# Prompt key and value rows of a hybrid decoder step stored from GpSimd's queue in place of the sync queue

## The chip, the cores and the metric

The kernel runs on one core of one Trainium2 chip. It is one launch of one inference step. The metric is the device time of the launch in microseconds (us): the median of several executions, 2409.1 us before the change (three runs, 2408.01 to 2414.72). One further execution was recorded by the profiler; the rows quoted below are from it. It took 2395.49 us.

The engines are called as in the profile: PE is TensorE (matrix products and transposes), DVE is VectorE, ACT is ScalarE, POOL is GpSimd and SP is SyncE. SP does no arithmetic here: it issues transfers (DMAs). POOL does both, in one stream of instructions: arithmetic, and the issue of its own transfers.

## The reference

The reference is one layer of a decoder for 256 prompt tokens and 8 x 4 new tokens of running samples. One input projection feeds two groups of heads (an RWKV-7 recurrence, and sparse attention with compressed, selected and window branches); an output projection and a layer norm follow, and then a mixer that picks experts by product keys, with a second layer norm. What matters here is that the keys and values of the prompt are outputs too:

```python
cuts = [D_NSA + i * NSA_KV_COLS for i in range(7)]
q, kc, vc, ksl, vsl, kw, vw, gl = jnp.split(xn, cuts, axis=-1)
kvh = lambda t: t.reshape(B, T, NSA_KV_HEADS, HEAD_DIM)
new_cmp = jnp.stack([kvh(kc), kvh(vc)], axis=2)
new_sel = jnp.stack([kvh(ksl), kvh(vsl)], axis=2)
new_win = jnp.stack([kvh(kw), kvh(vw)], axis=2)
...
return out, new_cmp, new_sel, win_pad[:, -n_keep:]
```

For each of the three branches a token has a row of 2 x 4 x 64 = 512 floats (keys, then values). For the prompt that is 3 x 256 rows; a block of 128 rows is 256 KB.

## The kernel before, in words

The projection makes the keys and values with columns in the partition dimension (tiles KT and KVT). `kv_rows` turns them into rows: for a token block t and a branch u it does four PE transposes into a PSUM bank (L590), one ACT copy of the bank to an SBUF tile of the ring `wraw` (L592; the ring has four buffers, which the weights of the projection use too), for the selected and the window branch a POOL copy of the values to VS or VW (L594), which the prompt's attention reads later, and the store of the row block to its output (L598). Blocks t = 0 and 1 are the prompt: 2 x 3 stores, six in all. The block of the samples (t = 2) goes out in small pieces at L602.

`kv_rows` is run by `attention_columns` and `new_keys`, in a weave with the second block of the prompt's RWKV steps (L1625). The weave is the order in which the program is written. The order in which each engine executes is chosen afterwards, when the kernel is built, by a scheduler that lays out all engines together by a timeline of its own; only some instructions are pinned (`keep_in_program_order`, `issue_after`). Each engine then runs its own list strictly in order, and an instruction that waits holds all that is behind it on its engine. Every transfer also takes one of eight completion semaphores, in turn, from a set of its kind: one set for SP's queue, one for POOL's. Before it is issued, the transfer that had that semaphore last must have landed.

Names that the prediction uses, in the order of time:

- L455, `gather`: POOL issues an indirect load of 128 rows. `co` tiles are blocks of the samples' compressed and selected cache (512 KB each), `cw` and `rows` are expert rows.
- L517, L522: POOL builds Qb, the samples' queries. L1190 and L1219: POOL's part in the RWKV steps of the prompt.
- L236, L1203, L1251, L1257 on SP: a table of constants (CT), the prompt's RWKV state going out, and the samples' RWKV inputs and states (S0T) coming in.
- From L1649 the samples' attention (`sample_attention`, 20 units: for each, key transposes L925, scores L944, softmax transposes L969, output product L988) is woven with the samples' RWKV steps (state transposes L1262 and L1349, products L1276, state update L1332 to L1344, with the POOL product `uvm` at L1339). It ends at about 746 us. The buffers of the gathered blocks come free when L988 of their unit has run.
- L1712 is the output projection. Its weights are split in a high and a low part (wh, wl; L1705 is the low one), and DVE adds its result to x (L1720). The first layer norm follows on DVE: statistics (L1721, L1770), the inverse root (L242 to L247), shift and scale (L1773), eight normed tiles (L1777), whose transposes on PE (L1780) open the query projection (L1873). Between these, DVE does L1600, products of gathered expert rows with the samples' tokens, and behind them L1796, gain and offset of the norm.

## Time and profile before

| | |
|---|---|
| median of three runs | 2409.1 us (2408.01 to 2414.72) |
| the profiled execution | 2395.49 us |
| its span (first to last instruction) | 2393.7 us |
| clock granted to PE, mean of the span | 0.967 of full speed |
| busy share of PE, DVE, POOL, ACT | 93%, 73%, 54%, 34% |
| SP's queue, POOL's queue | 341.93 MB and 338.78 MB |
| the six stores of L598 | 520.4 to 539.6 us, 1.5 MB |
| PE busy from 520 to 546 us | 25.86 of 26.00 us |
| PE busy from 546 to 746 us | 172.09 of 200.00 us |

The profile is one execution. A row of the timeline has a start, a duration, engine, line, operation, "output<-inputs" and, in brackets, how long the engine was idle just before and which instruction or transfer ended that idle time. A row of the waits has the waiting engine and line, then what it waited for, then the sum of the waits, their number and the longest. An x with a number behind a row is the number of instructions put together in it. Times are in us, durations of single instructions in groups are in ns. The profiled execution is 13.6 us faster than the median of the runs; differences that are worked out within the profile are therefore compared with its own time.

### The profile page before, as it was taken

The numbers are of one execution on the slowest core, as the hardware profiler recorded it, in microseconds if no ns is written. First come the engines' busy times: TensorE is split into PE (matmuls) and PEld (weight loads), VectorE is DVE, ScalarE is ACT, GpSimd is POOL, SyncE is SP. The second block draws the span as 40 slices with busy tenths as digits, with TensorE's granted clock in tenths as the row PEclk, the third lists the DMA queues.
The fourth block names the chain that finished last, engine by engine and source line by source line (L and its number), as shares of the span: only waits on it lengthen the run. The fifth ranks groups of instructions, "written<-read, shape, count | busy, mean of one in ns | idle before, by whom it ended". The sixth has DMA issues, their size and how long they took to land.

```text
span 2393.7 us, 42400 instructions
## 1 busy us (share of the span) xinstructions
PE 2222.6 (93%) x15564; PEld 1859.8 (78%) x15564; DVE 1758.0 (73%) x4041; ACT 824.4 (34%) x1609; POOL 1297.8 (54%) x1342
## 2 busy tenths in 40 slices
PE   7989999898989998699999999997998999999996
PEld 7877889896555665488888888886777888887885
DVE  5789866555664536889677776566877899998888
ACT  3433222223443433211111111113776444444343
POOL 5678522323454204467656654564442788876772
PEclk9999999998998998899999999998999999999998
DMA  7877985448667997799899999996663999999994
GB/s 218 234 228 244 268 238 169 130 140 257 215 238 264 292 321 257 275 354 376 314 375 374 377 391 345 386 403 219 187 196 109 346 356 362 362 363 349 354 357 177
DMA packets 311024, 683.42 MB, mean 286 GB/s; under 512 B 82238, under 2 KB 184576, under 8 KB 309888
## 3 DMA queue, kind: packets, MB, share of 16 engines
q1 hardware_dynamic: 229600, 341.93, 42.7%
q0 software_dynamic: 81216, 338.78, 39.2%
q8 instruction: 123, 2.02, 0.3%
q14 instruction: 85, 0.70, 0.1%
HBM read 665.04 MB, written 23.88 MB: 288 GB/s over the span
## 4 chain that ended last, share of the span: by engine, by line
PE 75%; DMA 8%; DVE 7%; POOL 3%; issue 3%; ACT 2%; SPq 1%; DVEq 0%; POOLq 0%; ACTq 0%
PE pb L2127 20%; PE ph L1919 19%; PE pj L424 8%; PE pj L1873 5%; PE px L1965 3%; PE pa L1712 3%; PE pa L1998 2%; DMA co<-in_cache_sel_kv,sidx 2%; PE p L1098 2%; PE pt L1957 2%; PE ss L1540 1%; PE fs L2017 1%; DMA co<-in_cache_cmp_kv,gidx 1%; DMA rows<-in_peer_u_g,gi 1%; PE sa L925 1%
## 5 line engine op out<-in xcount | busy, mean ns | idle before, releaser
L1919 PE MATMUL ph<-Xfd,ur 128*128 128x256 f32 x2304 | 497.6, 379 | 0.0
L1919 PEld LDWEIGHTS ph<-Xfd,ur 128*128 128x128 f32 x2304 | 437.6, 190 | 59.4
L455 POOL DMA_INDIRECT rq<-in_peer_v_g,gi x256 | 379.4, 1482 | 150.8 <-DVE fP L2100 90.0
L455 POOL DMA_INDIRECT rows<-in_peer_u_g,gi x256 | 303.3, 1185 | 202.7 <-DVE rows L1843 126.7
L1843 DVE SCALAR_TENSOR_TENSOR rows<-rows,x1a 128x896 f32<-128x896 f32 x256 | 279.4, 1099 | 141.5 <-DMA rows<-in_peer_u_g,gi 140.7
L424 PE MATMUL pj<-XH,wl 128*128 128x288 f32 (+1 forms) x752 | 230.8, 307 | 14.4 <-DVE wl L419 7.7
L424 PE MATMUL pj<-XH,wh 128*128 128x288 f32 (+1 forms) x752 | 228.6, 304 | 14.0 <-DVE ss L757 7.1
L2100 DVE SCALAR_TENSOR_TENSOR fP<-rq,ge,fP 128x640 f32<-128x640 f32 x254 | 223.9, 881 | 2.5
L424 PE MATMUL pj<-XL,wh 128*128 128x288 f32 (+1 forms) x752 | 225.0, 299 | 0.0
L2127 PE MATMUL pb<-vl,ah 128*128 128x512 f32 (+1 forms) x768 | 206.4, 377 | 0.8
L2127 PE MATMUL pb<-vh,al 128*128 128x512 f32 (+1 forms) x768 | 205.0, 375 | 0.0
L1920 ACT COPY AW<-ph 128x256 f32<-128x256 f32 x128 | 76.5, 614 | 363.9 <-PE ph L1919 351.2
L2127 PE MATMUL pb<-vh,ah 128*128 128x512 f32 (+1 forms) x768 | 186.7, 378 | 13.4 <-ACT vh L2119 10.9
L417 ACT CAST wh<-wraw 128x512 fp32r<-128x512 f32 (+1 forms) x188 | 114.7, 616 | 223.9 <-PE pj L424 160.0
L2127 PEld LDWEIGHTS pb<-vh,ah 128*128 128x128 f32 x768 | 144.8, 195 | 35.6 <-ACT vh L2119 13.9
L478 DVE SCALAR_TENSOR_TENSOR CA<-co,wbc,CA 128x256 f32<-128x256 f32 x248 | 136.5, 588 | 47.8 <-DMA co<-in_cache_cmp_kv,gidx 47.7
L424 PEld LDWEIGHTS pj<-XH,wl 128*128 128x128 f32 (+1 forms) x752 | 142.9, 190 | 26.5 <-DVE wl L419 12.1
L2127 PEld LDWEIGHTS pb<-vl,ah 128*128 128x128 f32 x768 | 144.6, 194 | 22.9 <-DVE vl L2120 3.8
L2127 PEld LDWEIGHTS pb<-vh,al 128*128 128x128 f32 x768 | 144.6, 194 | 19.2
L424 PEld LDWEIGHTS pj<-XH,wh 128*128 128x128 f32 (+1 forms) x752 | 143.1, 190 | 20.0 <-DVE ss L757 7.5
L424 PEld LDWEIGHTS pj<-XL,wh 128*128 128x128 f32 (+1 forms) x752 | 143.3, 191 | 1.5 <-issue 1.2
L419 DVE TENSOR_TENSOR wl<-wraw,wh 128x512 fp32r<-128x512 f32 (+1 forms) x141 | 101.3, 727 | 39.4 <-ACT wh L417 39.0
(867 smaller groups left out, 4252.5 us busy)
## 6 DMA issues: line engine op xcount, KB each, us to landing
ur<-in_peer_u_t SPq DMA_DIRECT2D x128, 576.0 KB
wraw<-in_w_in SPq DMA_DIRECT2D x152, 256.0 KB
cw<-in_w_out SPq DMA_DIRECT2D x32, 512.0 KB
wraw<-in_w_out SPq DMA_DIRECT2D x32, 512.0 KB
cw<-in_peer_wq SPq DMA_DIRECT2D x32, 512.0 KB
wraw<-in_peer_wq SPq DMA_DIRECT2D x32, 512.0 KB
wraw<-in_w_in SPq DMA_DIRECT2D x64, 128.0 KB
co<-in_state_win_kv SPq DMA_DIRECT2D x16, 512.0 KB
```

The lines of the kernel that those rows point to most:

```text
L417: sc.copy(wh[:, :, :n], w[:, :, :n])
L419: i_ = en.tensor_tensor(wl[:, :, :n], w[:, :, :n], wh[:, :, :n].bitcast(F32), OP.subtract)
L424: last[2] = pe.matmul(pb[:n, :nt], wi[:, k, :n], xi[(o + k) // 8][:, (o + k) % 8, :nt], start=(o + k == 0 and wi is wh and xi is xh), stop ...
L455: gp.indirect_dma_start(out=dst, out_offset=None, in_=rows_, in_offset=bass.IndirectOffsetOnAxis(ap=ix, axis=0))
L478: ve.scalar_tensor_tensor(d_, x_, w_, d_, op0=OP.mult, op1=OP.add)
L1712: pe.matmul(acc[t], xi[:, e, P * t:P * t + P], wi[:, e, :], start=(k == e == n_ == 0), stop=(k == 6 and e == 1 and n_ == 2))
L1843: i_ = ve.scalar_tensor_tensor(r_, r_, 1.0, X1a[t], op0=OP.mult, op1=OP.mult, accum_out=h_)
L1873: pe.matmul(pq[c][:, :NPR], w[:, k, 128 * c:128 * c + 128], XT[:, 4 * g + k, :], start=(g == k == 0), stop=(g == k == 3))
L1919: mm = pe.matmul(ph[:, :NPR], w[:, e, :], Xfd[:, e, :], start=(e == 0), stop=(e == NDB - 1))
L1920: return mm, sc.copy(AW[:, i1 // 64, :, i1 % 64], ph[:, :NPR])
L2100: ve.scalar_tensor_tensor(fP[t], r_, w_, fP[t], op0=OP.mult, op1=OP.add)
L2127: pe.matmul(acc[3 * t + q][:, :n_], wi[:, P * t:P * t + P], xi[:, 512 * q:512 * q + n_], start=(k == 0 and wi is ah and xi is vh), stop=(k ...
```

## The change

One line: the six stores are issued by POOL in place of SP. What they read, where they write and their size stay the same, and so does the waiting for ACT's copy of the row block.

```diff
             if t < 2:
                 o0 = 256 if u == 2 else 0
                 dst = outs[2 + u][0, 0].rearrange("t a h d -> t (a h d)")
-                sy.dma_start(dst[o0 + t * P:o0 + t * P + P, :], row_)
+                gp.dma_start(dst[o0 + t * P:o0 + t * P + P, :], row_)
             else:
```

In the lists of the engines more moves than the six stores, because the scheduler lays out everything that follows anew. Up to the place of the stores, all lists are the same.

First place, the stores themselves (some 519 to 545 us). POOL's list, a piece of the difference (- before, + now); `co` are gathers, `out` the stores:

```order
+L598 DMA out<-wraw 128x512
+L455 DMA co<-in_cache_sel_kv,sidx 128x1024
 L1190 TENSOR_TENSOR SBD_2479<-Sn,DT 64x4x64
 L1190 TENSOR_TENSOR SBD_3634<-Sn,DT 64x4x64
 L594 COPY vs_85<-wraw 128x256
+L598 DMA out<-wraw 128x512
 L594 COPY vw_87<-wraw 128x256
+L598 DMA out<-wraw 128x512 x2
 L594 COPY vs_86<-wraw 128x256
+L598 DMA out<-wraw 128x512
 L517 MEMSET Qb 128x512
```

The first store stands ahead of the fourth of the four gathers there; the second to fifth stand among the copies of L594, and ahead of Qb's memset. The rows that follow:

```order
-L522 COPY Qb<-QT 64x8x4
 L594 COPY vw_88<-wraw 128x256
-L522 COPY Qb<-QT 64x8x4 x15
+L598 DMA out<-wraw 128x512
+L522 COPY Qb<-QT 64x8x4 x16
 L1219 TENSOR_TENSOR YT_105<-YT_105,st_107 128x512
 L455 DMA co<-in_cache_sel_kv,sidx 128x1024 x10
```

The sixth store stands between the last L594 and the sixteen Qb copies, then L1219 and ten gathers. On SP the same six rows are gone, and the rows around them keep their order.

Second place, the samples' attention (546 to 746 us). PE's list at about 590 to 595 us, a piece of the difference:

```order
-L1276 MATMUL ss<-sS,S0T 64x8 x15
+L1276 MATMUL ss<-sS,S0T 64x8 x2
+L969 MATMUL st<-CT_61,S 128x128 x4
+L1276 MATMUL ss<-sS,S0T 64x8 x12
 L925 MATMUL sa<-CT_61,co 128x128 x6
-L969 MATMUL st<-CT_61,S 128x128 x4
```

The softmax transposes of one unit (L969) now stand ahead of key transposes (L925), where they stood behind them. PE's list at about 705 to 720 us before:

```order
L925 MATMUL sa<-CT_61,co 128x128 x6
L969 MATMUL st<-CT_61,S 128x128 x4
L925 MATMUL sa<-CT_61,co 128x128 x7
L1360 MATMUL ss<-Yq,CT_100 128x256
L925 MATMUL sa<-CT_61,co 128x128 x2
L988 MATMUL sao<-co,pt 32x128 x16
L969 MATMUL st<-CT_61,S 128x128 x4
L944 MATMUL sc<-kt,Qb 32x512 x4
L925 MATMUL sa<-CT_61,co 128x128
L988 MATMUL sao<-co,pt 32x128 x16
L969 MATMUL st<-CT_61,S 128x128 x4
L925 MATMUL sa<-CT_61,co 128x128 x6
```

And the same place now:

```order
L1349 MATMUL ss<-CT_61,S0T 128x128 x4
L988 MATMUL sao<-co,pt 32x128 x16
L969 MATMUL st<-CT_61,S 128x128 x4
L1349 MATMUL ss<-CT_61,S0T 128x128 x8
L988 MATMUL sao<-co,pt 32x128 x16
L969 MATMUL st<-CT_61,S 128x128 x4
L1349 MATMUL ss<-CT_61,S0T 128x128 x4
L1355 MATMUL ss<-Ya,CT_100 128x256
L988 MATMUL sao<-co,pt 32x128 x16
L925 MATMUL sa<-CT_61,co 128x128 x6
```

The state transposes (L1349), which before were all done by then, now stand between the units. POOL's list in the same stage, a piece of the difference; the gathers and the state products of L1339:

```order
 L1339 TENSOR_TENSOR uvm<-UB,CT_100 64x512 x2
 L455 DMA co<-in_cache_sel_kv,sidx 128x1024 x2
+L1339 TENSOR_TENSOR uvm<-UB,CT_100 64x512 x5
+L455 DMA co<-in_cache_sel_kv,sidx 128x1024 x4
 L1339 TENSOR_TENSOR uvm<-UB,CT_100 64x512 x2
 L455 DMA co<-in_cache_sel_kv,sidx 128x1024 x4
-L1339 TENSOR_TENSOR uvm<-UB,CT_100 64x512 x3
-L455 DMA co<-in_cache_sel_kv,sidx 128x1024 x10
+L1339 TENSOR_TENSOR uvm<-UB,CT_100 64x512
+L455 DMA co<-in_cache_sel_kv,sidx 128x1024 x6
```

More products than before now stand ahead of the last fourteen gathers: a run of five, then two and one, where it was two and three.

Third place, the first layer norm (some 994 to 1007 us). DVE's list before, around the inverse root (the rows of L242 to L246 ahead of the last round are between the two pieces):

```order
L1720 TENSOR_TENSOR x_11_9724<-x_11_9724,pa 128x512
L1770 BN_AGGR lnmv<-lnst 128x2
L1721 BN_STATS lnst<-x_11_9724 128x6
L1600 SCALAR_TENSOR_TENSOR cw,shT<-cw,x_10451 128x1024
L1770 BN_AGGR lnmv<-lnst 128x2
L1771 TENSOR_SCALAR lnv<-lnmv 128x2
L1600 SCALAR_TENSOR_TENSOR cw,shT<-cw,x_10451 128x1024
L242 TENSOR_SCALAR ln_t<-lnv 128x2
```

```order
L1600 SCALAR_TENSOR_TENSOR cw,shT<-cw,x_10451 128x1024
L245 TENSOR_TENSOR ln_t<-lnrr 128x2
L246 SCALAR_TENSOR_TENSOR ln_t<-ln_t,lnv 128x2
L1600 SCALAR_TENSOR_TENSOR cw,shT<-cw,x_10451 128x1024
L247 SCALAR_TENSOR_TENSOR lnrr<-ln_t,lnrr 128x2
L1773 SCALAR_TENSOR_TENSOR lnv<-lnmv,lnrr 128x2
L1600 SCALAR_TENSOR_TENSOR cw,shT<-cw,x_10451 128x1024
L1777 TENSOR_SCALAR x_00_9721<-x_00_9721,lnrr,lnv 128x512 x2
```

And now; the inverse root stands between the two pieces without a product in it:

```order
L1720 TENSOR_TENSOR x_01_9722<-x_01_9722,pa 128x512
L1600 SCALAR_TENSOR_TENSOR cw,shT<-cw,x_10451 128x1024
L1721 BN_STATS lnst<-x_01_9722 128x6
L1720 TENSOR_TENSOR x_11_9724<-x_11_9724,pa 128x512
L1600 SCALAR_TENSOR_TENSOR cw,shT<-cw,x_10451 128x1024
L1770 BN_AGGR lnmv<-lnst 128x2
L1721 BN_STATS lnst<-x_11_9724 128x6
L1600 SCALAR_TENSOR_TENSOR cw,shT<-cw,x_10451 128x1024
L1770 BN_AGGR lnmv<-lnst 128x2
```

```order
L247 SCALAR_TENSOR_TENSOR lnrr<-ln_t,lnrr 128x2
L1773 SCALAR_TENSOR_TENSOR lnv<-lnmv,lnrr 128x2
L1600 SCALAR_TENSOR_TENSOR cw,shT<-cw,x_10451 128x1024
L1777 TENSOR_SCALAR x_00_9721<-x_00_9721,lnrr,lnv 128x512 x2
```

Between the last addition to `x_01` (L1720) and the first L1777 there are four products of L1600 where there were five. Over the whole list the first L1777 has 20 of the 64 products ahead of it where it had 24; the last addition to `x_01` has 16 where it had 19.

## The prediction

> **What bounds the kernel now.** The page comes first: its head, and its chain of work that ended last.

> ```profile
> span 2393.7 us, 42400 instructions
> PE 2222.6 (93%) x15564; PEld 1859.8 (78%) x15564; DVE 1758.0 (73%) x4041; ACT 824.4 (34%) x1609; POOL 1297.8 (54%) x1342
> ...
> PE 75%; DMA 8%; DVE 7%; POOL 3%; issue 3%; ACT 2%; SPq 1%; DVEq 0%; POOLq 0%; ACTq 0%
> ```

> TensorE (PE) is busy 93% of the span and holds three quarters of the chain. A change elsewhere pays only where PE waits, so the second view is the table of busy time by stretch. Its columns are the stretch, its length, the busy time of PE, PEld, DVE, ACT and POOL, the clock that PE was granted, the DMA share and GB/s.

> ```profile
> 520.00:546.00 26.00, 25.86 (x385) 22.95 (x384) 10.55 (x22) 5.49 (x11) 8.47 (x26) 1.00 0.39 124
> 546.00:746.00 200.00, 172.09 (x1856) 109.24 (x1854) 123.80 (x446) 81.65 (x208) 79.05 (x86) 0.92 0.70 235
> 900.00:1014.00 114.00, 80.19 (x382) 60.71 (x370) 87.68 (x203) 32.96 (x64) 56.47 (x55) 0.82 0.78 273
> 1014.00:1160.00 146.00, 145.26 (x703) 128.43 (x704) 129.55 (x380) 22.61 (x57) 102.81 (x121) 1.00 0.94 340
> ```

> The six row stores fall in the first stretch. PE is idle for 26.00 - 25.86 = 0.14 us there: nothing in that place can be gained. The second (sample attention and the sample RWKV steps) leaves 200 - 172 = 28 us of PE idle, the third (end of the output projection and the first layer norm) 34 us; in the fourth PE is full again. What PE waited for there, in total, times, longest:

> ```profile
> PE sa L925 <- DMA co<-in_cache_sel_kv,sidx: 7.0, 9, 1.8
> PE sa L554 <- DVE gnt L246: 3.1, 1, 3.1
> PE sa L925 <- DMA co<-in_state_win_kv: 1.6, 1, 1.6
> ...
> PE pa L1780 <- DVE x L1777: 12.7, 1, 12.7
> PE pa L1712 <- DVE wl L1705: 6.9, 4, 3.3
> ```

> The first three rows are waits between 546 and 746, the last two between 880 and 1160. None names a store of L598.

> **The change, part by part.** *What leaves SP.* The instructions of L598 (durations in ns: shortest, median, longest; then first and last start), and the table of SP's waits from 510 to 600 (in total, times, longest):

> ```profile
> L598 SPq DMA_DIRECT2D out<-wraw x6: 332/332/361, 520.4 to 539.6; - x6
> ```

> ```profile
> SPq L598 <- ACT wraw L592: 14.8, 5, 8.7
> SPq L236 <- PE pb L590: 1.7, 1, 1.7
> SPq L1203 <- ACT So L1199: 0.9, 2, 0.5
> ```

> Six issues of 0.33 us, 2.0 us in all, nearly all of it inside the 14.8 us in which SP waits for ACT's row copies anyway. What stands behind them does not come earlier: the load of CT (L236) waits 1.7 us more for the PE transposes of the same rows, and the state stores behind it (L1203) wait for ACT. So SP gains at most the one issue of 0.33 us at 539.6, and I put this at 0.

> *What POOL gets.* POOL's timeline where the stores now stand (start, duration, what, and the idle time ahead with what ended it):

> ```profile
> 521.37 0.95 POOL L455 DMA_INDIRECT co<-in_cache_sel_kv,sidx  x1 [1.71 <-DVE CA L478]
> ...
> 529.60 0.39 POOL L594 COPY vs<-wraw 128x256 f32<-128x256 f32 x1 [2.88 <-ACT wraw L592]
> 532.23 0.40 POOL L594 COPY vw<-wraw 128x256 f32<-128x256 f32 x1 [2.23 <-ACT wraw L592]
> 536.78 0.40 POOL L594 COPY vs<-wraw 128x256 f32<-128x256 f32 x1 [4.16 <-ACT wraw L592]
> ...
> 540.05 3.14 POOL L522 COPY Qb<-QT 64x32 f32<-64x32 f32 x15
> 544.78 1.04 POOL L1219 TENSOR_TENSOR YT<-YT,st 128x512 f32<-128x512 f32 x1 [1.59 <-DVE st L1218]
> ...
> 554.79 0.95 POOL L455 DMA_INDIRECT co<-in_cache_sel_kv,sidx  x1 [0.30 <-DVE m L561]
> ```

> The price of an ordinary store that POOL issues, from the groups of instructions (busy us, mean ns | idle time ahead), and its time to landing from the list of DMA issues (count, size, us):

> ```profile
> L1797 POOL DMA_DIRECT2D x1d<-x x4 | 2.2, 559 | 16.9 <-DVE x L1796 16.9
> ...
> x1d<-x POOLq DMA_DIRECT2D x4, 512.0 KB, 9.0
> ```

> Six issues at 0.56 us are 3.4 us. By the order shown with the change, five stand in the idle time ahead of 538 (1.71 + 2.88 + 2.23 + 4.16 = 11.0 us, against 2.8 us). The sixth stands ahead of the Qb copies and moves them by 0.56 us; the 1.59 us of idle time in front of L1219 takes that up, so the ten gathers behind it keep their places. Without that cover the cost would be 0.56 us on the first gather. The stores of L598 also take turns on the eight completion semaphores that POOL's transfers share, so the fifth to eighth of the ten gathers now wait until the third to sixth store has landed. The last store goes out at about 540.6 and by the 9.0 us row has landed at 549.6, before the eighth gather at 554.79. I put POOL's side at 0, between -0.3 (SP's issue) and +0.6.

> How much can DVE hold up POOL's issue? The same kind of gather took two durations:

> ```profile
> 987.99 1.99 POOL L455 DMA_INDIRECT cw<-in_peer_u,gi  x1 [0.30 <-issue]
> ```

> Against 0.95 us at 521.37 this one took 1.04 us more, in a stretch in which DVE ran products of two SBUF operands (L1600) back to back. If each of the six stores met that, POOL would spend 6 x 1.60 = 9.6 us, still under the gaps; the sixth would push the Qb copies by 1.60 us, which is the 1.59 us of cover. So this bound too is about 0.

> [...]

> *What the order moves.* The program is laid out by a scheduler, and taking six issues from one queue changes what it writes for all engines behind 546. That is where a time can come from. Two places bear on rows.

> *Sample attention.* PE's rows between 705 and 720, in which the key transposes of L925 wait for gathered blocks:

> ```profile
> 708.96 0.98 PE L925 MATMUL sa<-CT,co 128*128 128x128 f32 x7 [1.36 <-DMA co<-in_cache_sel_kv,sidx]
> ...
> 718.39 1.54 PE L925 MATMUL sa<-CT,co 128*128 128x128 f32 x6 [1.77 <-DMA co<-in_cache_sel_kv,sidx]
> ```

> In the new order the transposes of the state (L1349), which wait for no gather, stand between the attention units there, so these two waits of 3.1 us are filled, if the gathers land when they did. Earlier, the softmax transposes of L969 come ahead of the window's key transposes (1.6 us of wait above), and DVE does the chain to L551 ahead of the norm chain (3.1 us of wait for gnt above); behind the latter PE soon waits for state loads, so I count none of it. Against it stands one unit whose output product comes some 2 us later. The ends are -28 us (all idle time of the stage) and, as POOL may lose there, +12 us (the third rival). I take 3.1 + 1.6 - about 1 for the late unit, some -4 us: the value is near the rows that the order touches, not near the ends.

> *First layer norm.* DVE's rows between the last additions of the projection and the normed tiles; PE waits through all of it (12.7 us):

> ```profile
> 993.81 0.69 DVE L1720 TENSOR_TENSOR x<-x,pa 128x512 f32<-128x512 f32 x1 [3.50 <-PE pa L1712]
> ...
> 996.46 1.21 DVE L1600 SCALAR_TENSOR_TENSOR cw<-cw,x 128x1024 f32<-128x1024 f32 x1
> ...
> 1002.24 1.23 DVE L1600 SCALAR_TENSOR_TENSOR cw<-cw,x 128x1024 f32<-128x1024 f32 x1 [1.57 <-DMA cw<-in_peer_u,ig]
> ...
> 1006.80 3.74 DVE L1777 TENSOR_SCALAR x<-x,lnrr,lnv 128x512 f32<-128x512 f32 x8
> ```

> Before, five sample products (L1600, 1.2 us each) stand between 996.46 and 1006.80, one of them with a wait of 1.57 us for its gather. In the new order four stand between the addition of 993.81 and L1777, and they are earlier ones of the series (the 17th to 20th, where before it was the 20th to 24th), whose rows were asked for earlier. That takes away one product, 1.2 us, and at most the 1.57 us of wait: -1.2 to -2.8, and I take -2. The four products put off run behind L1777, where DVE has 146 - 129.55 = 16 us of idle time for 4 x 1.2 = 4.8 us and PE is full; without that cover up to 4.8 us come back. Waits of PE for wl (6.9 us) may change too, since DVE does its L1705 among fewer products; I count 0, with 0 to -4 in the range.

> *Sum*: 0 (SP) + 0 (POOL) - 4 - 2 = -6 us. The profiled execution took 2395.5 us (span 2393.7), so 2389.5 us in such an execution; the median of the runs is 2409.1, 13.6 us above it, and the same -6 us on it gives 2403.

> **The rivals.** *Nothing moves* (2409 us): the stores do nothing on the path, and what the new order gains in one place it loses at the next transfer. For it: DMA is what ends many of the waits. That the change does not do what it says belongs here: the place of the stores had 0.14 us of PE idle time.

> *The new order gains more* (2391 us): half of the 28 us in the sample attention, plus 2.8 at the norm and 1 to 2 at wl, -18 us. Against it: what waits there waits mostly on gathers, whose times depend on PE's own progress (next rows).

> *POOL holds its gathers behind state products* (2419 us, slower). POOL's waits in 546 to 746, and one row of its timeline there:

> ```profile
> POOL co L455 <- PE sao L988: 66.5, 14, 13.1
> ...
> 668.24 1.04 POOL L1339 TENSOR_TENSOR uvm<-UB,CT 64x512 f32<-64x512 f32 x1 [5.95 <-PE ss L1341]
> ```

> Gathers go out as soon as PE's L988 gives a buffer back. In the new order a run of five uvm products (L1339) stands ahead of four gathers, then two ahead of four and one ahead of six; a product can wait 5.95 us for PE's L1341. Where PE's L988 is done before those products are, the gathers behind them are late by that wait. Two such groups, +12 us, less the 2 us of the norm: 2409 + 10 = 2419. It decides from the point at which L1341 comes later in PE's order than the L988 that frees the buffer. Against it: the scheduler lays out PE and POOL together, and POOL is idle 66.5 us for L988 in this stage.

> *DVE blocks the issue of the stores.* With the 1.04 us of the row above it is still covered; should the sixth issue take over 1.0 us more than its 0.56, the rest passes through the Qb copies and L1219 to the ten gathers, which slip by 1 or 2 us, and with them the L925 behind them: 2404 to 2405 with the order's gain, up to 2411 without it, nothing that can be told. [...]

> **How the numbers follow.** A measurement of this kernel can tell about 0.3% from no change, 7.2 us: under 2401.9 is faster, over 2416.3 slower. The forecast (2399 to 2407) has 0.42, of which 0.08 falls under 2401.9; nothing moves (2406 to 2412) 0.20; the order gains more (2388 to 2401) 0.22; POOL holds its gathers (2412 to 2428) 0.13 (all counted as slower); DVE blocks the issue 0.03. Faster: 0.08 + 0.22 = 0.30; slower 0.13; the same 0.57. The range leaves out the outer half of the gain rival and of the slower one: 2392 to 2419.

> **What would show it.** The six stores on POOL at 0.5 to 0.6 us each (2 us if DVE blocks them), L1219 and the ten gathers within 1 us of their old times, PE as full between 520 and 546; then fewer PE waits at L925 around 700 to 720, and L1777 some 2 us sooner after the last L1720, with PE's 12.7 us falling to about 10.7. Wrong it is if the ten gathers start over 1 us later, if POOL waits at L1339 with gathers behind it while PE's L925 waits rise over 7.0 us, or if the time moves in a stage whose order is the same.

## The result, and the profile after

The kernel with the change took 2427.6 us (median of six runs, 2423.1 to 2429.2), the kernel before 2414.5 us in six runs, the three shown ahead of the prediction among them: a ratio of 1.0065, with a 95% interval of 1.0047 to 1.0082. It is 13 us slower; the forecast was 6 us faster. In the two repeats below (the same kernel again, and its order with the old queue) the ratio was 1.003 and 1.005, so the loss lies between 0.3 and 0.7%.

The page of the changed kernel, its head and its chain:

```profile
span 2423.9 us, 42384 instructions
...
PE 2240.6 (92%) x15564; PEld 1868.7 (77%) x15564; DVE 1759.4 (73%) x4041; ACT 824.6 (34%) x1609; POOL 1309.9 (54%) x1348
...
PE 51%; DVE 2%; issue 2%; DMA 1%; ACT 1%; POOL 0%; SPq 0%; DVEq 0%; ACTq 0%; POOLq 0%
```

The chain could be followed over only 58% of the span, so its shares can't be set beside those of before. The span of before (2393.7 us) is a poor standard. Its execution was 13.6 us faster than the median, and when the kernel before was profiled again, its span was 2415.7, of which the sample attention alone took 211.6 us in place of 200.5. The second profile of before (the first experiment) is therefore used next to it. Against that one, PE did the same 15564 products and was busy 6.6 us longer (2240.6 and 2234.0). The table by stretch of the changed kernel (the stretch, its length, busy PE, PEld, DVE, ACT, POOL, the clock of PE, DMA share, GB/s), for the stores' place, the sample attention (from PE's first L525 to its first L631), the norm (from the last L1712 to the first L1873) and the query stage (from there to the first L1919):

```profile
524.00:550.00 26.00, 25.86 (x382) 22.84 (x379) 10.31 (x21) 5.48 (x11) 12.27 (x32) 1.00 0.39 125
550.10:770.10 220.00, 182.82 (x1855) 113.73 (x1854) 123.09 (x451) 82.20 (x210) 78.04 (x86) 0.86 0.65 214
1014.40:1031.60 17.20, 6.70 (x34) 6.07 (x32) 16.75 (x42) 6.05 (x18) 7.62 (x8) 0.70 0.68 229
1031.60:1161.00 129.40, 121.40 (x577) 106.48 (x578) 108.80 (x330) 18.64 (x49) 83.94 (x104) 0.96 0.97 349
```

And of the kernel before, in its second profile, with its own borders of the same stages:

```profile
526.40:552.40 26.00, 25.86 (x381) 22.81 (x379) 9.87 (x21) 5.30 (x10) 8.82 (x26) 1.00 0.40 122
552.40:764.10 211.70, 176.58 (x1855) 109.95 (x1854) 123.78 (x451) 82.57 (x210) 80.45 (x87) 0.91 0.66 222
1014.30:1034.70 20.40, 6.08 (x34) 5.48 (x32) 17.93 (x44) 6.07 (x18) 5.26 (x6) 0.67 0.76 275
1034.70:1152.80 118.10, 117.99 (x576) 104.42 (x577) 106.44 (x324) 18.56 (x48) 84.02 (x103) 1.00 0.98 359
```

At the stores PE is busy 25.86 us of 26.00 in both: the queue itself costs nothing. The sample attention is 8 us longer, with a clock of 0.86 in place of 0.91. The norm is 3 us shorter. The query stage, in which the prediction took PE to stay full, is 11 us longer and has lost its full clock. (The end of the output projection, from the last L1540 to the last L1712, went from 88.1 to 83.5 us.) The waits of the changed kernel that answer to those quoted of before:

```profile
POOL co L455 <- PE sao L988: 60.0, 13, 11.1
...
PE pa L1780 <- DVE x L1777: 9.6, 1, 9.6
...
PE sa L925 <- DMA co<-in_cache_sel_kv,sidx: 6.8, 4, 2.8
PE pj L1873 <- issue: 5.3, 1, 5.3
PE pa L1712 <- DVE wl L1705: 4.8, 4, 2.2
...
PE sa L554 <- DVE im L551: 3.2, 1, 3.2
...
PE sa L554 <- DVE s L548: 2.7, 1, 2.7
```

The norm's wait fell from 12.7 to 9.6 us, that for wl from 6.9 to 4.8. The gathers cost PE 6.8 us where they cost 7.0 (4.6 in the second profile of before): nothing was gained there. New are the 3.2 us at L554 and the 5.3 us at L1873.

*The stores.* The instructions of L598 on POOL, and POOL's timeline behind the last of them:

```profile
L598 POOL DMA_DIRECT2D out<-wraw x6: 539/550/631, 524.5 to 543.6; - x6
```

```profile
543.62 0.54 POOL L598 DMA_DIRECT2D out<-wraw  x1
544.16 3.48 POOL L522 COPY Qb<-QT 64x32 f32<-64x32 f32 x16
548.46 1.03 POOL L1219 TENSOR_TENSOR YT<-YT,st 128x512 f32<-128x512 f32 x1 [0.82 <-DVE st L1218]
549.66 1.02 POOL L455 DMA_INDIRECT co<-in_cache_sel_kv,sidx  x1 [0.16 <-issue]
```

L1219 still waits for DVE (0.82 us of its 1.59 us of idle time are left), so the sixth store moved nothing behind it. This is as predicted.

*The sample attention.* Between its 20 units the compressed branch has four units of its own (L537 to L577). PE's timeline of the changed kernel at the fourth of these:

```profile
684.67 1.07 PE L1341 MATMUL ss<-uvm,UB 64*64 64x512 f32 x4
686.19 0.66 PE L969 MATMUL st<-CT,S 128*128 128x128 f32 x4 [0.45 <-issue]
690.02 0.64 PE L554 MATMUL sa<-im,CT 128*128 128x32 f32 x2 [3.18 <-DVE im L551]
...
691.71 1.97 PE L1341 MATMUL ss<-uvm,UB 64*64 64x512 f32 x2
...
698.18 1.97 PE L925 MATMUL sa<-CT,co 128*128 128x128 f32 x8
700.08 1.97 PE L1341 MATMUL ss<-uvm,UB 64*64 64x512 f32 x2
701.97 1.93 PE L988 MATMUL sao<-co,pt 128*32 128x128 f32 x32
...
707.07 1.08 PE L1341 MATMUL ss<-uvm,UB 64*64 64x512 f32 x4
```

L554 turns the importance of the blocks into rows; DVE's chain L545 to L551 must be done first. PE waits 3.18 us for it, and then the same two products of L1341 take 1.97 us until about 705, and four of them 1.08 at 707. By the clock records PE was at half clock for 17.1 us, from 688.4 on, and behind L554 there is no idle time in them. The same place in the second profile of before:

```profile
688.06 1.08 PE L988 MATMUL sao<-co,pt 128*32 128x128 f32 x32
689.30 1.07 PE L1341 MATMUL ss<-uvm,UB 64*64 64x512 f32 x2 [0.16 <-POOL uvm L1339]
691.12 0.41 PE L554 MATMUL sa<-im,CT 128*128 128x32 f32 x2 [0.75 <-DVE im L551]
...
691.70 1.07 PE L1341 MATMUL ss<-uvm,UB 64*64 64x512 f32 x2
```

There an output product (L988) and two of L1341 stand between, PE waits 0.75 us, and L1341 goes on at 1.07.

*The query stage.* SP's timeline of the changed kernel, and PE's:

```profile
1035.39 3.83 SPq L1752 DMA_DIRECT2D wraw<-in_peer_wq  x2
1039.27 0.51 SPq L1862 DMA_DIRECT2D SKT<-in_subkeys_t  x1
1039.82 22.04 SPq L1752 DMA_DIRECT2D wraw<-in_peer_wq  x7
```

```profile
1031.64 14.08 PE L1873 MATMUL pj<-XT,wraw 128*128 128x256 f32 x64 [0.93 <-ACT XT L1783]
1048.26 1.13 PE L1387 MATMUL pb<-SKT,QP 128*128 128x128 f32 x8 [2.54 <-DMA SKT<-in_subkeys_t]
1054.72 20.58 PE L1873 MATMUL pj<-XT,wraw 128*128 128x256 f32 x81 [5.34 <-issue]
```

SKT holds the subkeys, 1 MB, which the scores L1387 need. Its load (L1862) now stands on SP behind two loads of query weights (L1752), which need ring buffers that PE frees only with its first L1873. SP's waits, over the whole span (in total, times, longest):

```profile
SPq L1752 <- PE pj L1873: 64.9, 14, 22.4
```

So the load goes out at 1039.27, 7.6 us after PE has begun the stage, and PE waits 2.54 us for it and then 5.34 us. For these the profile names nothing that ended them; in the repeat of the kernel the same wait (4.90 us) ended with a load of the weights that stand behind it. In the second profile of before it went out at 1012.9, 22 us ahead of PE's first L1873.

### The profile page after: what moved, and what is told of

It reads as the page before. It is cut to its first block, busy times and chain, and to the rows that moved or that the text cites. A ratio compares the mean times of both kernels' runs of the same rounds, so it can differ in the third digit from the quotient of the medians.

```text
span 2423.9 us, 42384 instructions
## 1 busy us (share of the span) xinstructions
PE 2240.6 (92%) x15564; PEld 1868.7 (77%) x15564; DVE 1759.4 (73%) x4041; ACT 824.6 (34%) x1609; POOL 1309.9 (54%) x1348
## 4 chain that ended last, share of the span: by engine, by line
PE 51%; DVE 2%; issue 2%; DMA 1%; ACT 1%; POOL 0%; SPq 0%; DVEq 0%; ACTq 0%; POOLq 0%
PE ph L1919 20%; PE pb L2127 18%; PE pj L1873 4%; PE px L1965 3%; PE pa L1998 2%; PE pt L1957 2%; PE fs L2017 1%; ACT vh L2119 1%; DVE vl L2120 1%; DMA rows<-in_peer_u_g,gi 1%; DMA wraw<-in_peer_wq 1%; DMA v__21674<-in_peer_v 0%; POOL rows L455 0%; PE pb L1387 0%; ACT XT L1783 0%
## 5 line engine op out<-in xcount | busy, mean ns | idle before, releaser
L1919 PE MATMUL ph<-Xfd,ur 128*128 128x256 f32 x2304 | 497.6, 379 | 0.0
L1919 PEld LDWEIGHTS ph<-Xfd,ur 128*128 128x128 f32 x2304 | 437.6, 190 | 59.4
L455 POOL DMA_INDIRECT rq<-in_peer_v_g,gi x256 | 385.6, 1506 | 146.0 <-DVE fP L2100 82.1
L455 POOL DMA_INDIRECT rows<-in_peer_u_g,gi x256 | 306.2, 1196 | 199.4 <-DVE rows L1843 118.4
L424 PE MATMUL pj<-XH,wh 128*128 128x288 f32 (+1 forms) x752 | 229.3, 305 | 12.7 <-DVE ss L757 5.9
L1920 ACT COPY AW<-ph 128x256 f32<-128x256 f32 x128 | 77.2, 609 | 397.9 <-PE ph L1919 358.1
L478 DVE SCALAR_TENSOR_TENSOR CA<-co,wbc,CA 128x256 f32<-128x256 f32 x248 | 134.3, 579 | 42.8 <-DMA co<-in_cache_cmp_kv,gidx 42.6
## 6 DMA issues: line engine op xcount, KB each, us to landing
cw<-in_w_out SPq DMA_DIRECT2D x32, 512.0 KB
wraw<-in_w_out SPq DMA_DIRECT2D x32, 512.0 KB
cw<-in_peer_wq SPq DMA_DIRECT2D x32, 512.0 KB
wraw<-in_peer_wq SPq DMA_DIRECT2D x32, 512.0 KB
co<-in_state_win_kv SPq DMA_DIRECT2D x16, 512.0 KB
```

The source lines that it names most:

```text
L424: last[2] = pe.matmul(pb[:n, :nt], wi[:, k, :n], xi[(o + k) // 8][:, (o + k) % 8, :nt], start=(o + k == 0 and wi is wh and xi is xh), stop ...
L455: gp.indirect_dma_start(out=dst, out_offset=None, in_=rows_, in_offset=bass.IndirectOffsetOnAxis(ap=ix, axis=0))
L478: ve.scalar_tensor_tensor(d_, x_, w_, d_, op0=OP.mult, op1=OP.add)
L1919: mm = pe.matmul(ph[:, :NPR], w[:, e, :], Xfd[:, e, :], start=(e == 0), stop=(e == NDB - 1))
L1920: return mm, sc.copy(AW[:, i1 // 64, :, i1 % 64], ph[:, :NPR])
```

## The experiments

In all but three, the order of every engine's list is fixed by hand. The scheduler gets an edge without a semaphore from each instruction to the next of the list wanted, so the order stays and no wait is added:

```diff
+        _pin(tc)
...
+                tc.add_manual_dep(i, last.name, mybir.DependencyInfo(mybir.DependencyClass.NoSync,
+                                  mybir.DependencyReason.DATA), reason="pin")
+            last = i
```

"Old order" is the lists of the kernel before, "new order" those of the changed one. Two things are told of each: the ratio to the kernel before on the same chip, and, from one profile, the length of the stage in question. Unit outputs are the L988 of the 20 attention units, counted from 0; the fourth compressed unit's L554 is between 11 and 12.

### Queue or order

The two kernels again, and the two crossings: old order with the stores on POOL, new order with the stores on SP.

```diff
 old order of every list
-                sy.dma_start(dst[o0 + t * P:o0 + t * P + P, :], row_)
+                gp.dma_start(dst[o0 + t * P:o0 + t * P + P, :], row_)
```

> The kernel before, unchanged, once more on the chip of the runs beside it, for a trace of the same session: the profile of before was taken at 2395 us and all six of its timed runs lie 13 to 22 us above that. Both theories expect a ratio of 1.000 to itself. If the trace is near 2414 us, part of the 30 us between the two spans seen so far belongs to the chip and not to the change; I expect 10 to 19 us of it to.

> The changed kernel, unchanged, beside the others. Both theories expect the ratio 1.0065 again (1.005 to 1.008), some 13 to 16 us over the kernel before.

> The six stores on GpSimd's queue at the places that the change gave them, and every other instruction of every engine pinned in the order of the kernel before. Theory O (the new order costs the time, the queue nothing): ratio 0.999 to 1.001, within 3 us of before. Theory Q (the stores cost on GpSimd's queue, by its time or by what the transfers meet): ratio 1.005 to 1.008, +13 to +16 us. Something between says that both have a part.

> The six stores on the sync queue at their old places, and every other instruction pinned in the order of the changed kernel. Theory O: ratio 1.005 to 1.008, as the changed kernel. Theory Q: 0.999 to 1.001, as the kernel before.

| run | order | stores | median us | ratio (95%) | sample attention | query stage |
|---|---|---|---|---|---|---|
| before again | old | SP | 2410.4 | 0.9987 (0.9966 to 1.0008) | 211.6 | 118.1 |
| old order, POOL stores | old | POOL | 2412.1 | 0.9991 (0.9968 to 1.0014) | 212.1 | 118.1 |
| after again | new | POOL | 2423.1 | 1.0030 (1.0001 to 1.0058) | 220.0 | 126.5 |
| new order, SP stores | new | SP | 2424.8 | 1.0049 (1.0023 to 1.0076) | 218.8 | 128.6 |

From the last L590, in the place of the stores, to the first L525 it was 7.8 us in all four. The queue makes no difference that can be measured; the order makes all of it. Both runs of the new order came out under the 1.005 to 1.008 that was expected.

### The subkeys' load

New order, with one row of SP's list moved back:

```diff
 L1768 DMA wraw<-in_ln_b 128x1024 x2
+L1862 DMA SKT<-in_subkeys_t 128x2048
 L1752 DMA wraw<-in_peer_wq 128x4x256 x2
-L1862 DMA SKT<-in_subkeys_t 128x2048
```

> The changed kernel with one row of the sync queue moved: the load of the subkeys (L1862) ahead of the two loads of the query weights (L1752), as before; all else pinned as in the changed kernel. Theory S (those two loads wait some 22 us for PE's first query products and hold the subkeys and the weights behind them): L1387 no longer waits for the subkeys, the stretch from the first L1873 to the first L1919 falls from 126.5 to 129.3 us to about 118 us, and the time by 8 to 11 us, to a ratio of 0.999 to 1.002. Rival D (the sample products put off behind the norm hold L1796, and so the buffers that the weights are loaded to): the stretch stays within 2 us of 128 us and the ratio at 1.003 to 1.006.

Measured: 2410.6 us, ratio 1.0000 (0.9981 to 1.0019); the query stage 118.4 us. SP's timeline, and PE's:

```profile
1015.60 0.43 SPq L1862 DMA_DIRECT2D SKT<-in_subkeys_t  x1
1038.65 18.79 SPq L1752 DMA_DIRECT2D wraw<-in_peer_wq  x9
```

```profile
1034.89 14.08 PE L1873 MATMUL pj<-XT,wraw 128*128 128x256 f32 x64 [1.64 <-ACT XT L1783]
1049.01 1.16 PE L1387 MATMUL pb<-SKT,QP 128*128 128x128 f32 x8
1050.00 20.89 PE L1873 MATMUL pj<-XT,wraw 128*128 128x256 f32 x96
```

The load goes out 19 us ahead of PE's first L1873, both waits are gone, and the weights behind come in time too. One row of one list was worth 8 to 11 us of the stage.

### The importance chain on DVE

New order, with DVE's state updates behind the chain:

```diff
 L548 RECIPROCAL s_8836<-s_8836 128x1
+L549 TENSOR_SCALAR Pn<-Pn,s_8836 128x64
+L551 TENSOR_TENSOR im<-Pn 128x32
 L1343 TENSOR_TENSOR S0T<-ss,S0T 128x8x64
-L549 TENSOR_SCALAR Pn<-Pn,s_8836 128x64
 L1344 TENSOR_TENSOR S0T<-S0T,sS 128x8x64
-L551 TENSOR_TENSOR im<-Pn 128x32
```

> The changed kernel with two rows of VectorE moved: in the fourth compressed unit, the two updates of the samples' state (L1343, L1344) that stand within the importance chain go behind it (behind L551); all else pinned as in the changed kernel. Theory G (PE's wait of 3.2 us at L554, 135 to 138 us after the first L525, sets off the 17 us at half clock that follow): the wait falls below 1.5 us, the spell shrinks to 7 us or less, and the stretch from the first L988 to the first L631 falls by 4 to 8 us from 195 to 197. Rival N (the half clock there comes of something else, such as what kind of products run): the wait falls by 2 us, the spell stays at 14 to 17 us, and the stretch falls by 2 us or less. The ratio falls by 0.001 (N) to 0.003 (G).

Measured: 2416.9 us, ratio 1.0022 (1.0004 to 1.0040). The wait at L554 fell only from 3.2 to 2.7 us, the half clock behind it stayed 17 us, and unit output 11 to 12 took 17.9 us, where the changed kernel takes 18.4. That DVE's order is the cause of the wait is a miss. (From the first L988 to the first L631 it took 188.8 us, 6 to 8 us less than the three runs of the new order, as theory G foretold. But the wait and the spell were as before, and about half of this was gained ahead of output 11, so it is not the theory's doing.)

What holds the chain is one instruction, L549, which scales the probabilities. DVE's timeline there and POOL's beside it, of the changed kernel:

```profile
687.29 1.98 DVE L549 TENSOR_SCALAR Pn<-Pn,s 128x64 f32<-128x64 f32 x1
687.16 2.04 POOL L1339 TENSOR_TENSOR uvm<-UB,CT 64x512 f32<-64x512 f32 x2
```

And of the kernel before, in its second profile:

```profile
689.37 0.93 DVE L549 TENSOR_SCALAR Pn<-Pn,s 128x64 f32<-128x64 f32 x1
688.21 2.03 POOL L1339 TENSOR_TENSOR uvm<-UB,CT 64x512 f32<-64x512 f32 x2 [0.22 <-PE ss L1341]
```

At the other three compressed units, with no such product beside it, L549 takes 0.24 to 0.38 us. At the fourth it begins within the second of two products of L1339 in the old order and takes 0.93 us; in the new order it begins within the first and takes 1.98. In all 17 profiles it ends 0.05 to 0.06 us behind the product. In the run with the updates moved (1.35 us of work) L549 took 2.44 us, so the chain gained little. From the end of L542 to L554 it is 5.3 us in the changed kernel and 4.0 before, and 1.05 us of the difference is L549; PE has 1.7 us of work in that time where it had 3.1. No run moved POOL's products, so that they hold DVE is read from these rows and was not tried.

### Old order up to a border, new order behind it

> The changed kernel with all engines pinned in the order of before up to the end of the samples' attention (the first L631 of PE), and in the order of the changed kernel from there. If the losses and gains of the two orders sit where the traces put them (+10 us in the attention, -3.5 in the projection, -3.2 at the norm, +10 in the query stage), it is 10 us faster than the changed kernel and 2 to 4 us slower than before: ratio 1.001 to 1.002. If the loss of the query stage is an after-effect of the attention's delay, it is gone as well: ratio 0.996 to 0.998.

> As the run beside it (old order up to the first L631, new order from there), and the load of the subkeys ahead of the two loads of the query weights. By theory S and the sums by stretch: -3.5 in the projection, -3.2 at the norm, nothing lost: 6 to 7 us faster than before, ratio 0.996 to 0.998. By rival D: as the run beside it, 1.001 to 1.002.

Both have the stores on POOL and the old lists up to the end of the sample attention; the second also has SKT's row ahead as above. Measured: 2416.6 us, ratio 1.0033 (1.0011 to 1.0054), and 2404.5 us, 0.9970 (0.9951 to 0.9988). In the same session, the one row is worth 12 us (query stage 129.2 and 118.4). The second is **faster than both kernels**: it has the old attention, and behind it what the new order gives (projection's end 83.6 us, norm 11.0). Unit output 11 to 12 took 6.6 us in both. The first is over the 1.001 to 1.002 that was expected. In its profile it had a spell of 37.5 us at half clock early in its attention, where its order is the old one. Such spells come and go between executions: the whole attention in the old order took 200.5, 211.6, 212.1, 217.8 and 208.6 us in five profiles, so that its length in one profile tells little.

> All engines in the changed kernel's order up to the fourth compressed unit (the seventh L537 of PE, some 133 us after the first L525), and in the order of before from there to the end. Theory P (the attention's loss sits behind that place; ahead of it the new order costs nothing): 183 to 189 us from the first L988 to the first L631, ratio 0.998 to 1.001. Rival E (the loss comes of the earlier part, and is only paid later): 193 to 197 us, ratio 1.003 to 1.005.

> The reverse: the order of before up to that place, the changed kernel's order from there, with the subkeys' load first. Theory P: the loss is there, 192 to 197 us from the first L988 to the first L631; with the gains of projection and norm (-6.7) the ratio is 0.999 to 1.002, as b1. Rival E: 183 to 189 us, ratio 0.996 to 0.998, as b4.

Here the border is in the middle of the sample attention, at the seventh L537, ahead of the place in question. Measured: new, then old 2413.0 us, ratio 1.0018 (1.0002 to 1.0034); old, then new with SKT ahead 2408.6 us, 0.9997 (0.9975 to 1.0019). Unit output 11 to 12 took 10.7 us in the first and 18.4 in the second, which also had the 17 us at half clock. The second shows that the loss comes with the new order of this place even where all ahead of it is old, as theory P has it. The first is a miss for theory P: from the first L988 to the first L631 it took 195.3 us, which is what the rival foretold, and its ratio lies between the two. From output 10 to 12, across the border, it took 19.7 us, with 10.3 to 12.0 in the old order and 22.8 to 23.6 in the new one. So it is not shown that the old order from there on takes the loss away; the join of the two orders may have a price of its own.

### The wait at L554 and the half clock

New order with SKT ahead, and two products of L1341 moved into the wait (PE's list):

```diff
 L969 MATMUL st<-CT_61,S 128x128 x4
+L1341 MATMUL ss<-uvm,UB 64x512 x2
 L554 MATMUL sa<-im,CT_141 128x32
```

> The changed kernel with the subkeys' load first (as in b1) and with two state products (L1341) moved on PE from behind L554 of the fourth compressed unit to just ahead of it, into the 3.2 us in which PE waits there; nothing else moved. Theory G (that wait sets off the 14 to 17 us at half clock behind it): idle time ahead of L554 falls from 3.2 to 1.3 to 1.8 us, L554 itself comes no more than 0.5 us later, the spell shrinks to 7 us or less, the stretch from the twelfth to the thirteenth output product (18 us in the new order, 6.8 in the old) falls to 13 us or less, and the ratio to 0.996 to 0.998. Rival N (the spell comes of something else): the spell stays at 14 to 17 us, the stretch falls by 1 to 2 us, ratio 0.999 to 1.000.

Measured: 2404.7 us, ratio 0.9980 (0.9965 to 0.9996). The wait became two of 1.4 and 0.5 us, the half clock behind it 6.8 us, unit output 11 to 12 took 14.5 us. But this moves work too, so one more run fills the wait with work that is of no use, and two others repeat the controls:

```diff
-            for k in range(4):
+            for k in (0, 1, 2, 3) * (5 if i == 12 else 1):
```

> The changed order with the subkeys' load first (as in the run with the keys' load first), plus 16 more transposes of L969 in one unit of the sample attention: they repeat the four that stand just ahead of the importance step of the fourth compressed unit and write the same values again, useless work of about 2.2 us which PE does in the 3.2 us that it otherwise waits at L554. Theory 'the gap sets off the half clock': the wait at L554 falls to 1 us or less, the spell at half clock behind it (13.7 us in the earlier run of this order with the keys' load first) falls to 7 us or less, the stretch from unit output 11 to unit output 12 falls from 17.7 to 13 to 14.5 us, and the time is 3 to 7 us below its control's. Rival 'the spell comes from the work itself': the wait falls in the same way, the spell stays at 13 to 17 us, the stretch stays at 17 to 18.5 us, and the time is within 2 us of its control's.

> The control of the run before it, the changed order with the subkeys' load first, once more on this chip. Both theories: unit output 11 to 12 in about 18 us, a wait of some 3.2 us at L554 and 13 to 17 us at half clock behind it; ratio to the kernel before 0.999 to 1.002.

> The same order with two products of L1341 moved ahead of the fourth L554, once more on this chip. Theory 'the gap sets off the half clock': as in its first run, a wait of 1.4 to 1.9 us, a spell of about 7 us, 14 to 15 us from unit output 11 to 12, ratio 0.996 to 0.999. Rival: the first run was luck, the spell is 13 us or more and the ratio that of the control.

| run | median us | ratio (95%) | unit output 11 to 12 | half clock behind L554 |
|---|---|---|---|---|
| wait filled | 2407.2 | 0.9990 (0.9964 to 1.0015) | 12.9 | none |
| control | 2415.6 | 1.0006 (0.9988 to 1.0024) | 18.4 | 17.1 |
| L1341 early | 2407.8 | 0.9991 (0.9972 to 1.0011) | 13.6 | 6.8 |

PE's timeline of the run with the wait filled, and of its control:

```profile
687.25 2.40 PE L969 MATMUL st<-CT,S 128*128 128x128 f32 x20 [0.44 <-issue]
691.09 0.41 PE L554 MATMUL sa<-im,CT 128*128 128x32 f32 x2 [1.44 <-DVE im L551]
...
692.01 1.07 PE L1341 MATMUL ss<-uvm,UB 64*64 64x512 f32 x2
```

```profile
687.21 0.66 PE L969 MATMUL st<-CT,S 128*128 128x128 f32 x4 [0.44 <-issue]
691.06 0.64 PE L554 MATMUL sa<-im,CT 128*128 128x32 f32 x2 [3.19 <-DVE im L551]
...
692.74 1.97 PE L1341 MATMUL ss<-uvm,UB 64*64 64x512 f32 x2
```

From L969 to L554 both take 3.8 us, so the filling made nothing earlier. All that differs is what comes behind. The table by stretch for the 17 us behind L554, of the run with the wait filled and of its control:

```profile
691.09:708.09 17.00, 16.50 (x178) 9.44 (x178) 12.46 (x35) 5.39 (x13) 10.68 (x11) 1.00 0.48 167
```

```profile
691.06:708.06 17.00, 17.00 (x99) 8.81 (x99) 6.98 (x25) 2.40 (x6) 5.78 (x6) 0.55 0.19 67
```

The control does 99 products in the 17 us, with PE busy all the time, and the other 178. The work behind L554 is the same in both, so the idle time of 3.2 us, and not that work, sets off the spell at half clock: useless work saves 5.5 us from one unit output to the next. This is one profile of each. The medians differ by 8.4 us; the intervals of the ratios overlap, so the effect on the whole time rests on the stage, not on them.

### Another queue

With the scheduler free, the six stores on ACT's queue:

```diff
-                sy.dma_start(dst[o0 + t * P:o0 + t * P + P, :], row_)
+                sc.dma_start(dst[o0 + t * P:o0 + t * P + P, :], row_)
```

> The kernel before with the six stores issued by ScalarE's queue, and the scheduler free to lay out the rest as it comes out. The lists change as much as in the change (291 lines of PE's differ from before, 937 of VectorE's). Theory O (the queue costs nothing; what counts is how the lists fall out): the stores' place costs under 1 us (first L590 to first L525 as before), and the time differs from before by some -10 to +15 us, made in the attention, the projection and the query stage, ratio 0.996 to 1.006. Theory Q (an engine's queue costs as such): ScalarE, which has a third of its time busy, pays less than GpSimd, and the ratio lies at 1.000 to 1.002 with the loss between 520 and 560 us.

Measured: 2412.0 us, ratio 1.0025 (1.0005 to 1.0046), though its profiled execution had a span of 2402.3. Each issue took 0.34 us. The order came out as a third one: unit output 11 to 12 in 6.6 us as in the old order, projection's end and norm as short as in the new one (83.4 and 10.2 us), and 123.0 us in the query stage, between the two. Nothing in its profile accounts for a median above that of before; this stays open.

## Why the prediction was wrong

*SP 0 and POOL 0*: right. The crossings show it: with the old order, stores on POOL give 0.9991. The six issues took 0.54 to 0.63 us against the 0.56 taken, and the ten gathers began at the old distance from L1219. The rival that DVE blocks the issue did not happen: no store took over 0.63 us. DVE worked beside four of the six (L478 and L1171 beside the first, L1171 beside the fourth and fifth, L1185 beside the sixth), and these took 0.63, 0.54, 0.54 and 0.54 us; beside the second and third it was idle, and they took 0.63 and 0.56. No run shows the slip of 1 or 2 us that this rival puts on the ten gathers: the sixth issue left 0.82 us of idle time ahead of L1219. Nor does the gather of 1.99 us give a price for L1600: in the same profile one at 979.86 us, which ran wholly beside L1600, took 0.94.

*First layer norm -2*: right in mechanism, with four L1600 ahead of L1777 in place of five. It was -3.1 (12.7 to 9.6 us at L1780; 9.5 to 10.6 in other runs of the new order), near its bound of -2.8. *wl, counted 0 with -4 at most*: the projection's end gained 3.2 to 4.6 us in the new order (88.1 to between 83.5 and 84.9), of which 2.1 at wl (6.9 to 4.8 us); the rest was not taken apart. So the gains were bigger than forecast, some 7 us. The four products put off behind L1777 did not come back: with SKT ahead, the query stage takes 118.4 us with them.

*Sample attention -4*: **this step failed**. It came out at some +8: 210 us in the mean of the five profiles of the old order named above, and 218 in five of the new one (220.0, 220.0, 218.8, 215.6 and 217.5). The part from unit output 11 to the end is steadier, 75.0 to 77.7 us in the old order and 81.2 to 86.8 in the new one. The gain at L925 and at the first L554 hardly came: the waits for gathers were 6.8 us, with 7.0 and 4.6 before, and 2.7 us of the 3.1 at L554 are still there, now for L548. The loss is at a place that the prediction did not read. It said that DVE's chain to L551 comes ahead of the norm chain at one unit, and did not ask what each of the other units' L554 has ahead of it on PE. At the fourth, L988 and two L1341 had gone from between, L549 took 1.05 us more beside POOL's products (which the prediction weighed for the gathers alone), and a wait of 0.7 us became one of 3.2. And a wait was priced at its own length. Behind this one PE ran up to 17 us at half clock, which cost 5.5 us more up to unit output 12 (shown by the filled wait). Whether all of that lasts to the end of the attention is not shown: from output 11 on it took 81.1 us with the wait filled and 84.8 in its control, but the control's kernel took 81.2 in its first profile, with the wait and 13.7 us at half clock. The wait itself counts 2.4 us (3.2 less 0.75). What else is in the loss was not taken apart.

*The sum left a term out*: SP's list had L1862 two rows later, and this was not priced. It cost 8 to 11 us in the query stage. The working looked at SP only around the stores, and took "the rows around them keep their order" for the whole list. A load that stands behind two others is late by as long as those wait for a buffer: it went out 7.6 us behind PE's first L1873, and with its row moved back 19.3 us ahead of it.

*By the terms*: +8 (attention), +11 (subkeys), -3 (norm), -4 (projection's end) is +12 us, against 13 between the medians. That they agree so well is in part luck: the two profiles that the terms are from differ by 8.2 us, since the changed kernel was 2.3 us faster ahead of the attention, where the lists are the same but for the stores, and 1.3 us between the attention and the projection's end; in the repeat the medians differ by 9.6. Some 5 us of the distance between forecast and result are not of the change: the kernel before took 2414.5 us in the median of all six runs and 2409.1 in the three shown.

*The rivals.* "Nothing moves" holds for the queue and not for the order. "POOL holds its gathers" ended on the right side for another reason: POOL's wait for L988 was 60.0 us, with 66.5 and 77.2 before, and PE's waits for the gathers stayed under the 7.0 us that were named as its sign. The gain of the third case is there in part, in the run with the old attention and SKT ahead (0.9970).

## What to carry to other kernels

Where a scheduler lays out the program, an edit of one transfer is an edit of every list behind it: price each row that changed place on a queue of loads by what it now stands behind, to the end of the program, before the place that the diff names. A load with a free destination should not stand behind loads that wait for a ring buffer (8 to 11 us here). A wait of PE of some 3 us has to be priced with the clock behind it (17.1 us at half behind the 3.2 us at L554), so that filling it with anything, useless work too, can pay (5.5 us up to the next unit output here). And where a short instruction of DVE stands in a chain that PE waits for, look at what POOL does beside it (L549 took 1.98 us beside two products of POOL, and 0.25 to 0.37 at the other units).

## What the runs showed of the hardware

Other waits of that length did not cost the same. A wait of 2.8 us at an L969 in the old order was followed by a single step, in the second profile of before; 3.1 us at the first L554 of the old order by one or two; and 2.7 to 2.8 us at the first L554 of the new order by one step in six profiles and by five in four. What decides how long the clock stays low was not found.

An instruction of DVE of 0.25 us (L549) that met a product of POOL (L1339, 1.0 us each) ended 0.05 to 0.06 us behind it, behind both where two followed each other, in all 17 profiles, and so took 0.92 to 2.45 us.
